# Mamba-2 mixer, two-layer decoder: the steps that read a projection's finished PSUM bank get a scheduling priority of 60

## The chip, the cores and the metric

One Trainium2 chip; the kernel runs on one core. The metric is the device time of the whole kernel in microseconds (us), the median over several runs; lower is better. TensorE (PE) multiplies matrices into PSUM, VectorE (DVE) and ScalarE (ACT) work element by element on PSUM and SBUF, GpSimd (POOL) on SBUF, and SyncE (SP) issues most DMAs.

## The reference

A two-layer decoder trunk, 2048 tokens of width 1024, float32. Layer 1 is a Mamba-2 mixer, layer 2 latent attention, each with a residual add; a final norm follows. Only the mixer bears on the change:

```python
proj = h @ w_in
z, xBC, dt_raw = jnp.split(proj, [D_INNER, D_INNER + CONV_DIM], axis=-1)
xBC = jax.nn.silu(causal_depthwise_conv(xBC, conv_w, conv_b))
...
y = ssd_chunked_scan(xh, dt, A, Bm, Cm)          # 4 groups of 8 heads, chunk by chunk
y = y + D_skip[:, None] * xh
y = y * jax.nn.silu(z)
y = y * lax.rsqrt(jnp.mean(y * y) + EPS) * g_out  # the mean per group
return y @ w_out                                  # added to h
```

D_INNER is 2048 and the groups are 4, so the mixer has an input projection of 1024 to 5152 columns and an output projection of 2048 to 1024.

## The kernel before

**Tiling.** The tokens are cut into 4 blocks of 512 (b) and the inner width into 4 groups of 512 (g). `mamba()` walks the 16 items (b, g). For an item it runs the scan `ssd(b, g)` in four chunks of 128 tokens, and beside it, as generators that are stepped in turn with the scan's 20 steps, the projections that surround it: `outp` of the item before (its output projection), `xbc` (the convolution's input) and `zgate` (the gate) of the next item. So the projections' matmuls fill TensorE while the scan's chain of small steps runs on the other engines.

**A projection.** `sweep()` fills banks of PSUM, tag "mm", of which there are four in all. For each product of two 128-row factors `mm3` (L401, L402, L403) issues three f16 or fp32r matmuls (high x high, high x low, low x high). The first two products run bank by bank, the middle ones product by product, and the last two bank by bank again; right after a bank's last matmul `evacuate(bank, i)` is called. The next projection's first matmul into a bank must wait until `evacuate` has read it. There are three such functions:

- in `xbc`, L1054: a ScalarE copy (with a scale) of the bank into `craw`; GpSimd saves three columns (L1055), ScalarE and VectorE compute the convolution into `cacc` (L1058, three times L1060) and the SiLU into `xs` or `BC` (L1062, L1063)
- in `zgate`, L1089 and L1090: a ScalarE Tanh of the bank into `sz`, then a VectorE product of `sz` and the bank
- in `outp`, L1119: a VectorE product of the bank and `rr`, added to the residual `hs`. `outp` does this twice, for the column halves n = 0 and n = 1; at the boundary between the two the four banks of n = 0 are read by four such steps, and n = 1 starts into the same banks.

**The scan's steps, per chunk.** `big` holds the decay matrix E (loaded by a DMA, L1235 and L1236 on ScalarE); VectorE multiplies it by `CB` (L1237) and makes `Xd` (L1245, with a priority of 20) and the first part of `y` (L1248) from the transposed `xs` (L1242 on TensorE). ScalarE makes `Xw` (L1251), ScalarE and GpSimd `Xp` (L1206, L1207). Then TensorE computes L1258 (32 small matmuls from `Xd` and `big`) and L408 to L410 (from `Sp`, `Ct` and from `Xp`, `Bt`). PSUM tag "tr" serves these, with four banks of its own.

**What sets the order.** A tile scheduler puts every instruction into its engine's queue. It goes by priority, which is the place in the program's text, and by its own estimate of when operands are there; an engine then works its queue in order. Inside `with tc.high_priority(n)` instructions get a priority of n places further ahead. Before the change the weights' loads and splits (`wunit`, `wpair`, `opair`: ScalarE L439, VectorE L440) have 10 (`AHEAD`) and `Xd` has 20.

Of the kernel before, what the change touches and what calls it, by code (L numbers as in the profile page):

```python
# [16 lines left out]
AF = mybir.ActivationFunctionType  # L17
ALU = mybir.AluOpType
# [366 lines left out]
class Net:  # L385
# [631 lines left out]
    def xbc(self, b, g):  # L1017

        nc, w_in, xT = self.nc, self.a["ssm_w_in"], self.xT[b]
        outs = []  # L1020
        for chans, tag, bufs in (([16 + g, 20 + g], "BC", 4), ([4 * g + j for j in range(4)], "xs", 8)):
            banks = [self.t(self.pp, "mm", [P, TB], bufs=4) for _ in chans]

            def load(k, raw):
                rows = slice(k * P, (k + 1) * P)
                if tag == "xs":
                    nc.sync.dma_start(raw, w_in[rows, DI + g * 512:DI + (g + 1) * 512])
                else:
                    both = w_in[rows, DI + DI:DI + DI + 1024].rearrange("p (n q c) -> p n q c", n=2, q=G)
                    nc.sync.dma_start(raw[:, :256].rearrange("p (n c) -> p n c", n=2), both[:, :, g, :])  # L1030

            def weights(k):
                n = 512 if tag == "xs" else 256
                if b:
                    return self.wpair(b, g, 1024 if tag == "xs" else 2048, n, k, load)
                with self.tc.high_priority(AHEAD):
                    raw = self.t(self.wp, "wraw", [P, TB], bufs=WRAW)
                    load(k, raw)
                    w = self.t(self.wp, "wsp", [P, 2, TB], F32R, bufs=WSP)
                    w = [w[:, i, :n] for i in range(2)]  # L1040
                    at = 3 * g + (1 if tag == "xs" else 2)
                    nc.scalar.activation(w[1], raw[:, :n], AF.Square, accum_out=self.nrm[:, k, at:at + 1])
                    self.split(*w, raw[:, :n])
                return w

            def product(bank, k, i, w, start, stop):
                s = slice(i * P, (i + 1) * P)
                self.mm3(bank, w[0][:, s], w[1][:, s], xT[k][:, 0, :], xT[k][:, 1, :], start, stop)

            def evacuate(bank, i):  # L1050
                ch = chans[i]
                raw = self.t(self.sp, "craw", [P, TB + 3], bufs=3)
                nc.gpsimd.tensor_copy(raw[:, 0:3], self.halo[:, ch, :])
                nc.scalar.activation(raw[:, 3:], bank, AF.Copy, scale=self.un if b else 1.0)  # L1054
                nc.gpsimd.tensor_copy(self.halo[:, ch, :], raw[:, TB:TB + 3])  # L1055
                acc = self.t(self.sp, "cacc", [P, TB], bufs=2)
                wk = [self.cw[:, 4 * ch + k:4 * ch + k + 1] for k in range(4)]
                nc.scalar.activation(acc, raw[:, 0:TB], AF.Identity, scale=wk[0], bias=self.cb[:, ch:ch + 1])  # L1058
                for k in range(1, 4):
                    nc.vector.scalar_tensor_tensor(acc, raw[:, k:k + TB], wk[k], acc, ALU.mult, ALU.add)  # L1060
                o = self.t(self.sp, tag, [P, TB], bufs=bufs)
                nc.scalar.activation(o, acc, AF.Tanh)  # L1062
                nc.vector.scalar_tensor_tensor(o, o, 1.0, acc, ALU.add, ALU.mult)  # L1063
                outs.append(o)

            yield from self.sweep(KD, banks, weights, product, evacuate)
        self.conv[b, g] = outs

    def zgate(self, b, g):

        nc, xT = self.nc, self.xT[b]
        banks, out = [self.t(self.pp, "mm", [P, TB], bufs=4) for _ in range(4)], []

        def load(k, raw):
            nc.sync.dma_start(raw, self.a["ssm_w_in"][k * P:(k + 1) * P, g * 512:(g + 1) * 512])

        def weights(k):
            if b:
                return self.wpair(b, g, 0, 512, k, load)
            return self.wunit(self.a["ssm_w_in"][k * P:(k + 1) * P, g * 512:(g + 1) * 512], 512,  # L1080
                              norm=self.nrm[:, k, 3 * g:3 * g + 1])

        def product(bank, k, i, w, start, stop):
            s = slice(i * P, (i + 1) * P)
            self.mm3(bank, xT[k][:, 0, s], xT[k][:, 1, s], *w, start, stop)

        def evacuate(bank, i):
            sz = self.t(self.sp, "sz", [P, TB], bufs=SZ)
            nc.scalar.activation(sz, bank, AF.Tanh, scale=self.unh if b else 0.5)  # L1089
            nc.vector.scalar_tensor_tensor(sz, sz, 1.0, bank, ALU.add, ALU.mult)  # L1090
            out.append(sz)

        yield from self.sweep(KD, banks, weights, product, evacuate)
        self.sz[b, g] = out

    def outp(self, b, g):

        nc, a, t0 = self.nc, self.a, b * TB
        if g == 0:
            self.hs[b] = [self.t(self.hh, "hs", [P, D], bufs=4) for _ in range(4)]  # L1100
            for i in range(4):
                nc.sync.dma_start(self.hs[b][i], a["x"][t0 + i * P:t0 + (i + 1) * P, :])
        hs, yT, rr = self.hs[b], self.yT.pop((b, g)), self.rr.pop((b, g))
        for n in range(2):
            banks = [self.t(self.pp, "mm", [P, TB], bufs=4) for _ in range(4)]

            def weights(j):
                if b:
                    return self.opair(b, g, n, j)
                r0, at = g * 512 + j * P, 4 * g + j  # L1110
                return self.wunit(a["ssm_w_out"][r0:r0 + P, n * 512:(n + 1) * 512], 512,
                                  self.go[:, at:at + 1], self.nrmw[:, 2 * at + n:2 * at + n + 1])

            def product(bank, j, i, w, start, stop):
                self.mm3(bank, yT[i][:, 0, j, :], yT[i][:, 1, j, :], *w, start, stop)

            def evacuate(bank, i):
                hv = hs[i][:, n * 512:(n + 1) * 512]
                nc.vector.scalar_tensor_tensor(hv, bank, rr[:, i:i + 1], hv, ALU.mult, ALU.add)  # L1119

            yield from self.sweep(4, banks, weights, product, evacuate)
        if g == G - 1:
            for i in range(4):
                nc.sync.dma_start(self.h_d[t0 + i * P:t0 + (i + 1) * P, :], hs[i])
# [832 lines left out]
```

## Time and profile before

| what | value |
| --- | --- |
| median of 3 runs | 2937.92 us (2934.6 to 2940.88) |
| the profiled run's own time | 2937.34 us |
| span of the profiled execution | 2935.6 us |
| mean granted TensorE clock | 0.993 |
| mixer | about 0 to 1640 us of the span |
| TensorE busy in the mixer | 1554.33 of 1640 us |
| VectorE, ScalarE busy in the mixer | 1276.16, 1088.72 us |

The profile is one execution. A row of the timeline gives the start in us, the duration, the engine, the line, the operation, output and inputs, and in brackets how long the engine stood before it and for what. Matmuls are pipelined, so their durations overlap: in a row of them each starts 0.215 us after the one before, although a row shows 0.38. Also on VectorE a next instruction starts a little before the row of the one before ends; the start-to-start distance is what an instruction takes of the queue. A view of waits gives, for a line, what it waited for, the total, the number of times and the longest.

### The profile page before, as it was taken

Reading aid. Unit: us, or ns where it says so; the run is one execution under the profiler, and the core shown is the slowest. Engines: PE = TensorE matmul, PEld = TensorE weight load, DVE = VectorE, ACT = ScalarE, POOL = GpSimd, SP = SyncE. Lnnn points to the kernel's source line nnn. Section 1 sums busy time; section 2 is a strip of 40 time slices with the busy share of each in tenths; the row PEclk is TensorE's granted clock in tenths of the full one; section 3 lists DMA queues with packets and bytes.
Section 4 is the critical chain, followed back from the end, with each engine's and each line's share of the span. In section 5 each row is a group of like instructions: output and inputs, shape, how many; then the busy total and the mean of one; then the engine's idle time right before and its main releaser. Section 6 shows DMA issues by size and latency. Waiting matters only on the chain.

```text
span 2935.6 us, 48796 instructions
## 1 busy us (share of the span) xinstructions
PE 2818.1 (96%) x16346; PEld 1652.4 (56%) x16346; DVE 2195.7 (75%) x4751; ACT 1865.0 (64%) x4728; POOL 987.4 (34%) x1200
## 2 busy tenths in 40 slices
PE   7999999989999999999999999999999999998998
PEld 6787755444444444444455555454555555554687
DVE  6778888888877777788766653644888889887575
ACT  7888777665766555566554442433888888887322
POOL 1222112212111221221111221222888888878300
PEclk9999999999999999999999999999999999999999
DMA  6333346656557545476444765555999999998894
GB/s 186 91 118 97 103 157 219 193 175 195 169 155 245 160 123 153 125 227 192 132 145 131 250 198 171 177 184 181 180 182 179 181 191 183 175 200 176 197 273 146
DMA packets 602144, 507.56 MB, mean 173 GB/s; under 512 B 413954, under 2 KB 455938, under 8 KB 601892
## 3 DMA queue, kind: packets, MB, share of 16 engines
q1 hardware_dynamic: 590020, 466.03, 60.8%
q0 software_dynamic: 11872, 38.41, 3.7%
q8 instruction: 128, 2.10, 0.3%
q14 instruction: 124, 1.02, 0.1%
HBM read 303.37 MB, written 104.47 MB: 139 GB/s over the span
## 4 chain that ended last, share of the span: by engine, by line
PE 60%; DVE 15%; ACT 8%; DMA 7%; issue 6%; POOL 3%; SPq 1%; ACTq 0%; POOLq 0%; DVEq 0%
PE mm L401 11%; PE mm L403 11%; PE mm L402 11%; PE tr L401 4%; PE tr L1717 4%; PE tr L403 4%; PE tr L402 4%; DVE cacc L1060 4%; DMA wraw<-in_ssm_w_in_dram 2%; PE mm L1690 2%; PE mm L1717 1%; PE tr L1258 1%; DMA big<-cumT 1%; PE tr L1690 1%; DVE wsp L440 1%
## 5 line engine op out<-in xcount | busy, mean ns | idle before, releaser
L1682 POOL TENSOR_TENSOR HL<-Pr,HL 128x512 f16<-128x512 f32 x320 | 371.0, 1159 | 25.5
L401 PE MATMUL mm<-xT,wsp 128*128 128x512 f16 (+1 forms) x800 | 309.5, 387 | 6.7 <-DVE sz L1090 5.1
L402 PE MATMUL mm<-xT,wsp 128*128 128x512 f16 (+1 forms) x800 | 307.2, 384 | 0.0
L403 PE MATMUL mm<-xT,wsp 128*128 128x512 f16 (+1 forms) x800 | 306.1, 384 | 0.7 <-DVE wsp L432 0.5
L1207 POOL TENSOR_TENSOR Xp<-Xw,Xp 128x512 fp32r<-128x512 f32 x64 | 87.2, 1363 | 561.6 <-ACT Xp L1206 538.6
L1676 ACT ACTIVATE Pr<-mm,nm 128x512 f32<-128x512 f32 (+3 forms) x356 | 221.1, 625 | 65.1 <-DVE nm L1671 52.9
L1665 DVE TENSOR_REDUCE mx<-mm 128x1 f32<-128x512 f32 (+3 forms) x356 | 211.6, 608 | 32.5 <-PE mm L403 18.2
L401 PE MATMUL mm<-wsp,xT 128*128 128x512 f16 (+2 forms) x640 | 233.6, 366 | 1.1 <-ACT craw L1054 0.6
L402 PE MATMUL mm<-wsp,xT 128*128 128x512 f16 (+2 forms) x640 | 233.2, 365 | 1.0 <-DVE wsp L440 1.0
L403 PE MATMUL mm<-wsp,xT 128*128 128x512 f16 (+2 forms) x640 | 232.9, 364 | 0.0
L1060 DVE SCALAR_TENSOR_TENSOR cacc<-craw,pack,cacc 128x512 f32<-128x512 f32 x288 | 220.6, 784 | 11.6 <-ACT cacc L1058 9.9
L1681 POOL CAST HL<-Pr 128x512 f16<-128x512 f32 x320 | 196.2, 613 | 95.1 <-ACT Pr L1676 94.1
L401 PE MATMUL mm<-wsp,yT 128*128 128x512 f16 (+1 forms) x512 | 199.0, 389 | 15.3 <-ACT craw L1054 8.0
L1235 ACT ACTIVATE big<-big,d_cum 128x128 f32<-128x128 f32 x512 | 169.7, 391 | 52.0 <-DMA big<-cumT 51.9
L402 PE MATMUL mm<-wsp,yT 128*128 128x512 f16 (+1 forms) x512 | 197.4, 386 | 0.3 <-DVE wsp L440 0.3
L403 PE MATMUL mm<-wsp,yT 128*128 128x512 f16 (+1 forms) x512 | 196.9, 385 | 0.0
L403 PEld LDWEIGHTS <-xT 128*128 128x128 f16 (+1 forms) x1280 | 124.7, 97 | 117.5 <-issue 2.9
L402 PEld LDWEIGHTS <-xT 128*128 128x128 f16 (+1 forms) x1280 | 125.6, 98 | 112.5 <-issue 16.9
L401 PEld LDWEIGHTS <-xT 128*128 128x128 f16 (+1 forms) x1280 | 125.1, 98 | 108.9 <-issue 17.4
L1251 ACT ACTIVATE Xw<-tr,d_wend 128x64 f32<-128x64 f32 x512 | 112.1, 328 | 111.1 <-DVE y L1248 98.2
L1676 ACT ACTIVATE Pr<-tr,nm 128x512 f32<-128x512 f32 (+3 forms) x284 | 174.1, 618 | 8.9 <-DVE nm L1671 7.9
L1665 DVE TENSOR_REDUCE mx<-tr 128x1 f32<-128x512 f32 (+3 forms) x284 | 166.1, 596 | 17.8 <-PE tr L1650 13.6
(504 smaller groups left out, 7552.7 us busy)
## 6 DMA issues: line engine op xcount, KB each, us to landing
wsp<-w_d SPq DMA_DIRECT2D x68, 512.0 KB, 3.8
wraw<-in_ssm_w_in_dram SPq DMA_DIRECT2D x128, 256.0 KB, 3.1
big<-cumT SPq DMA_DIRECT2D x64, 512.0 KB, 4.2
wraw<-in_ssm_w_out_dram SPq DMA_DIRECT2D x64, 256.0 KB, 3.1
w_d<-wsp SPq DMA_DIRECT2D x32, 512.0 KB, 3.5
wsp<-wo_d SPq DMA_DIRECT2D x32, 512.0 KB, 4.1
st<-w_d SPq DMA_DIRECT2D x56, 256.0 KB, 2.9
wsp<-wu_d SPq DMA_DIRECT2D x28, 512.0 KB, 3.8
```

The source lines that it names most:

```text
L401: mm(out, l_hi, r_hi, start=start, stop=False)
L402: mm(out, l_hi, r_lo, start=False, stop=False)
L403: mm(out, l_lo, r_hi, start=False, stop=stop)
L1060: nc.vector.scalar_tensor_tensor(acc, raw[:, k:k + TB], wk[k], acc, ALU.mult, ALU.add)
L1235: act(E[:, h, :], E[:, h, :], AF.Relu, bias=ncum[:, h0 + h:h0 + h + 1])
L1251: act(Xw[:, hc], px[:, hc], AF.Copy, scale=wend[:, h0 + h:h0 + h + 1])
L1665: v.tensor_reduce(m[:, at:at + 1], s, AX.X, ALU.max, negate=True)
L1676: nc.scalar.activation(tile("Pr", n, j, c)[:, :w], bank("S", n, j, c)[:, :w], AF.Exp, bias=moves[(4 * n + j) % len(moves)], accum_out=sums ...
L1681: nc.gpsimd.tensor_copy(u[:, 0], x)
L1682: nc.gpsimd.tensor_tensor(u[:, 1], x, u[:, 0], ALU.subtract)
L1690: nc.tensor.transpose(bank("T", n, k)[:, j * P:(j + 1) * P], tile("Pr", n, j, k // 4)[:, k % 4 * P:(k % 4 + 1) * P], self.ident)
L1717: nc.tensor.matmul(o, weights, half(n, k, low), start=start, stop=not left[n][at[0]])
```

## The change

The steps that read the bank are put in `high_priority(60)`: the ScalarE copy of the convolution's input, the Tanh and the product of the gate, the residual. Nothing else of the functions is touched, and no computing instruction is added or removed, only semaphore events change. Lines behind the change have numbers 1 to 3 higher (L1119 is now L1122, L1237 L1240, L1245 L1248, L1258 L1261).

```diff
--- before.py
+++ after.py
@@ -1051,7 +1051,8 @@
                 ch = chans[i]
                 raw = self.t(self.sp, "craw", [P, TB + 3], bufs=3)
                 nc.gpsimd.tensor_copy(raw[:, 0:3], self.halo[:, ch, :])
-                nc.scalar.activation(raw[:, 3:], bank, AF.Copy, scale=self.un if b else 1.0)
+                with self.tc.high_priority(60):
+                    nc.scalar.activation(raw[:, 3:], bank, AF.Copy, scale=self.un if b else 1.0)
                 nc.gpsimd.tensor_copy(self.halo[:, ch, :], raw[:, TB:TB + 3])
                 acc = self.t(self.sp, "cacc", [P, TB], bufs=2)
                 wk = [self.cw[:, 4 * ch + k:4 * ch + k + 1] for k in range(4)]
@@ -1086,8 +1087,9 @@
 
         def evacuate(bank, i):
             sz = self.t(self.sp, "sz", [P, TB], bufs=SZ)
-            nc.scalar.activation(sz, bank, AF.Tanh, scale=self.unh if b else 0.5)
-            nc.vector.scalar_tensor_tensor(sz, sz, 1.0, bank, ALU.add, ALU.mult)
+            with self.tc.high_priority(60):
+                nc.scalar.activation(sz, bank, AF.Tanh, scale=self.unh if b else 0.5)
+                nc.vector.scalar_tensor_tensor(sz, sz, 1.0, bank, ALU.add, ALU.mult)
             out.append(sz)
 
         yield from self.sweep(KD, banks, weights, product, evacuate)
@@ -1116,7 +1118,8 @@
 
             def evacuate(bank, i):
                 hv = hs[i][:, n * 512:(n + 1) * 512]
-                nc.vector.scalar_tensor_tensor(hv, bank, rr[:, i:i + 1], hv, ALU.mult, ALU.add)
+                with self.tc.high_priority(60):
+                    nc.vector.scalar_tensor_tensor(hv, bank, rr[:, i:i + 1], hv, ALU.mult, ALU.add)
 
             yield from self.sweep(4, banks, weights, product, evacuate)
         if g == G - 1:
```

What the scheduler makes of it: on VectorE 73 of the 128 residuals and 12 of the 64 gate products move forward, 23 of 64 `Xd` and 25 of 64 `big` move back; on ScalarE 47 of 96 copies and 13 of 64 Tanh move forward. TensorE's order changes where VectorE's does.

**VectorE at the boundary from n = 0 to n = 1 of the item at 600 to 611 us of the profile (block 1).** `hs` with the four numbers is the four residuals, `cacc` and `xs` the next item's convolution, `Xd`, `big` and `y` the scan's chunk. Before:

```order
L1060 SCALAR_TENSOR_TENSOR cacc_6398<-craw_6394,pack,cacc_6398 128x512
L1245 TENSOR_TENSOR Xd_6480<-tr_6475,d_dt_3869 128x512
L1063 SCALAR_TENSOR_TENSOR xs_6385<-xs_6385,cacc_6380 128x512
L1060 SCALAR_TENSOR_TENSOR cacc_6398<-craw_6394,pack,cacc_6398 128x512
L1237 TENSOR_TENSOR big_6440<-big_6440,CB_6451 128x1024
L1060 SCALAR_TENSOR_TENSOR cacc_6398<-craw_6394,pack,cacc_6398 128x512
L1248 TENSOR_TENSOR y_6483<-tr_6475,pack 128x512
L1119 SCALAR_TENSOR_TENSOR hs_6406<-mm_6414,rr_5918,hs_6406 128x512
L1063 SCALAR_TENSOR_TENSOR xs_6403<-xs_6403,cacc_6398 128x512
L1119 SCALAR_TENSOR_TENSOR hs_6407<-mm_6415,rr_5918,hs_6407 128x512
L1119 SCALAR_TENSOR_TENSOR hs_6408<-mm_6416,rr_5918,hs_6408 128x512
L1119 SCALAR_TENSOR_TENSOR hs_6409<-mm_6417,rr_5918,hs_6409 128x512
```

After:

```order
L1122 SCALAR_TENSOR_TENSOR hs_6406<-mm_6414,rr_5918,hs_6406 128x512
L1064 SCALAR_TENSOR_TENSOR xs_6385<-xs_6385,cacc_6380 128x512
L1061 SCALAR_TENSOR_TENSOR cacc_6398<-craw_6394,pack,cacc_6398 128x512
L1122 SCALAR_TENSOR_TENSOR hs_6407<-mm_6415,rr_5918,hs_6407 128x512
L1061 SCALAR_TENSOR_TENSOR cacc_6398<-craw_6394,pack,cacc_6398 128x512
L1122 SCALAR_TENSOR_TENSOR hs_6408<-mm_6416,rr_5918,hs_6408 128x512
L1236 TENSOR_TENSOR CB_6451<-tr_6442,pack 128x128
L1064 SCALAR_TENSOR_TENSOR xs_6403<-xs_6403,cacc_6398 128x512
L1122 SCALAR_TENSOR_TENSOR hs_6409<-mm_6417,rr_5918,hs_6409 128x512
L1248 TENSOR_TENSOR Xd_6480<-tr_6475,d_dt_3869 128x512
L1240 TENSOR_TENSOR big_6440<-big_6440,CB_6451 128x1024
```

The four residuals stood behind `Xd`, `big` and `y`, and now stand ahead of them.

**TensorE at the same place.** `mm_1184` is the last bank of n = 0, `mm_1204` to `mm_1207` are the banks of n = 1, `tr_1201` is the scan's L1258 and `tr_1202` its L408 to L410. Before:

```order
L403 LDWEIGHTS yT_1023_5539
L403 MATMUL mm_1184_6417<-wsp_1197_6493,yT_1023_5539 128x512
L1258 MATMUL tr_1201_6534<-Xd_1194_6480,big_1188_6440 64x64 x16
L408 MATMUL tr_1202_6552<-Sp_1159_6299,Ct_1191_6448 128x512
L409 MATMUL tr_1202_6552<-Sp_1159_6299,Ct_1191_6448 128x512
L410 MATMUL tr_1202_6552<-Sp_1159_6299,Ct_1191_6448 128x512
L401 LDWEIGHTS yT_952_5138
L401 MATMUL mm_1204_6559<-wsp_1208_6563,yT_952_5138 128x512
L402 LDWEIGHTS yT_952_5138
```

After, the last rows of the third bank of n = 1 and what follows it:

```order
L402 LDWEIGHTS yT_1023_5539
L402 MATMUL mm_1206_6561<-wsp_1208_6563,yT_1023_5539 128x512
L403 LDWEIGHTS yT_1023_5539
L403 MATMUL mm_1206_6561<-wsp_1208_6563,yT_1023_5539 128x512
L1261 MATMUL tr_1201_6534<-Xd_1194_6480,big_1188_6440 64x64 x16
L408 MATMUL tr_1202_6552<-Sp_1159_6299,Ct_1191_6448 128x512
L409 MATMUL tr_1202_6552<-Sp_1159_6299,Ct_1191_6448 128x512
L410 MATMUL tr_1202_6552<-Sp_1159_6299,Ct_1191_6448 128x512
L401 LDWEIGHTS yT_1023_5539
```

L1258 (now L1261) stood at the boundary itself; now the 18 matmuls of the banks `mm_1204`, `mm_1205` and `mm_1206` stand between the last matmul of n = 0 and it.

**VectorE at the next item's boundary, 702 to 708 us.** The names are as in the first place. Before:

```order
L1063 SCALAR_TENSOR_TENSOR xs_7418<-xs_7418,cacc_7413 128x512
L1060 SCALAR_TENSOR_TENSOR cacc_7431<-craw_7427,pack,cacc_7431 128x512
L1233 TENSOR_TENSOR CB_7498<-tr_7489,pack 128x128
L1060 SCALAR_TENSOR_TENSOR cacc_7431<-craw_7427,pack,cacc_7431 128x512
L1237 TENSOR_TENSOR big_7487<-big_7487,CB_7498 128x1024
L1063 SCALAR_TENSOR_TENSOR xs_7436<-xs_7436,cacc_7431 128x512
L1119 SCALAR_TENSOR_TENSOR hs_6406<-mm_7449,rr_6916,hs_6406 128x512
L1245 TENSOR_TENSOR Xd_7553<-tr_7548,d_dt_3869 128x512
L1119 SCALAR_TENSOR_TENSOR hs_6407<-mm_7450,rr_6916,hs_6407 128x512
L1119 SCALAR_TENSOR_TENSOR hs_6408<-mm_7451,rr_6916,hs_6408 128x512
```

After:

```order
L1061 SCALAR_TENSOR_TENSOR cacc_7431<-craw_7427,pack,cacc_7431 128x512
L1061 SCALAR_TENSOR_TENSOR cacc_7413<-craw_7409,pack,cacc_7413 128x512
L1122 SCALAR_TENSOR_TENSOR hs_6406<-mm_7449,rr_6916,hs_6406 128x512
L1061 SCALAR_TENSOR_TENSOR cacc_7431<-craw_7427,pack,cacc_7431 128x512
L1064 SCALAR_TENSOR_TENSOR xs_7418<-xs_7418,cacc_7413 128x512
L1122 SCALAR_TENSOR_TENSOR hs_6407<-mm_7450,rr_6916,hs_6407 128x512
L1064 SCALAR_TENSOR_TENSOR xs_7436<-xs_7436,cacc_7431 128x512
L1122 SCALAR_TENSOR_TENSOR hs_6408<-mm_7451,rr_6916,hs_6408 128x512
L1122 SCALAR_TENSOR_TENSOR hs_6409<-mm_7452,rr_6916,hs_6409 128x512
L432 TENSOR_TENSOR Bt_7492<-tr_7489,Bt_7492 128x128
L1236 TENSOR_TENSOR CB_7498<-tr_7489,pack 128x128
L1248 TENSOR_TENSOR Xd_7553<-tr_7548,d_dt_3869 128x512
```

The first residual stood behind `CB` and `big` and now stands ahead of both and of `Bt`, with the other three between `xs` and `cacc`; `Xd` and `big` come after all four.

**VectorE near 428 to 440 us.** `wsp` is a weight pair's split for the gate; the pair has a first split from one `wraw` and a second from the next. Before, the pair's two splits:

```order
L440 SCALAR_TENSOR_TENSOR wsp_4715<-wraw_4716,rw,wsp_4715 128x512
L1063 SCALAR_TENSOR_TENSOR xs_4568<-xs_4568,cacc_4563 128x512
L1060 SCALAR_TENSOR_TENSOR cacc_4581<-craw_4577,pack,cacc_4581 128x512
L440 SCALAR_TENSOR_TENSOR wsp_4715<-wraw_4720,rw,wsp_4715 128x512
L1060 SCALAR_TENSOR_TENSOR cacc_4581<-craw_4577,pack,cacc_4581 128x512
```

After, the second of them (from `wraw_4720`):

```order
L1248 TENSOR_TENSOR Xd_4702<-tr_4697,d_dt_310 128x512
L1064 SCALAR_TENSOR_TENSOR xs_4615<-xs_4615,cacc_4610 128x512
L1064 SCALAR_TENSOR_TENSOR xs_4633<-xs_4633,cacc_4628 128x512
L1240 TENSOR_TENSOR big_4662<-big_4662,CB_4673 128x1024
L1251 TENSOR_TENSOR y_4705<-tr_4697,pack 128x512
L440 SCALAR_TENSOR_TENSOR wsp_4715<-wraw_4720,rw,wsp_4715 128x512
```

The second split stood two places behind the first in the middle of the convolution, and now stands behind `Xd`, `xs`, `big` and `y`.

## The prediction

> **What bounds the kernel now.** I read the page first: the share of each engine, then the chain that ended last.
>
> ```profile
> PE 2818.1 (96%) x16346; PEld 1652.4 (56%) x16346; DVE 2195.7 (75%) x4751; ACT 1865.0 (64%) x4728; POOL 987.4 (34%) x1200
> PE 60%; DVE 15%; ACT 8%; DMA 7%; issue 6%; POOL 3%; SPq 1%; ACTq 0%; POOLq 0%; DVEq 0%
> ```
>
> TensorE is busy 96% of 2935.6 us, so what an order can win is the time in which it stands. The change touches the mixer alone, about 0 to 1640 us. The view of waits for TensorE from 60 to 1500 us (columns: instruction, what it waited for, us in total, times, longest) gives the prices:
>
> ```profile
> PE tr L410 <- POOL Xp L1207: 12.9, 18, 1.4
> PE tr L1258 <- DVE big L1237: 10.7, 6, 2.5
> PE mm L401 <- ACT craw L1054: 8.5, 7, 2.8
> PE tr L1258 <- issue: 7.6, 6, 2.5
> PE mm L401 <- DVE hs L1119: 7.0, 4, 3.3
> PE mm L401 <- DVE sz L1090: 5.1, 4, 2.3
> PE tr L1258 <- DVE Xd L1245: 3.8, 4, 1.6
> ```
>
> Three rows are the change's target, a projection that waits for a bank to be read: 8.5 + 7.0 + 5.1 = 20.6 us, 0.7% of the span. That is the ceiling of the direct gain. Three others are the scan's products (L1258), which wait for Xd and big: 10.7 + 7.6 + 3.8 = 22.1 us. These operands come from the engine that the residuals use, VectorE, and they are what the change puts behind.
>
> **The boundary between the two halves of an output projection.** There the four residuals of n = 0 free the banks of n = 1, and a chunk's L1258 stands nearby. At 607 us the timeline shows this, and the windows view the load of the 28 us around it:
>
> ```profile
> 604.68 0.38 PE L403 MATMUL mm<-wsp,yT 128*128 128x512 f16 x1
> 605.04 0.75 DVE L1060 SCALAR_TENSOR_TENSOR cacc<-craw,pack,cacc 128x512 f32<-128x512 f32 x1
> 605.71 1.22 DVE L1237 TENSOR_TENSOR big<-big,CB 128x1024 f32<-128x1024 f32 x1
> 606.84 0.74 DVE L1060 SCALAR_TENSOR_TENSOR cacc<-craw,pack,cacc 128x512 f32<-128x512 f32 x1
> 607.03 1.15 PE L1258 MATMUL tr<-Xd,big 128*64 128x64 f32 x32 [1.97 <-issue]
> 608.11 0.74 DVE L1119 SCALAR_TENSOR_TENSOR hs<-mm,rr,hs 128x512 f32<-128x512 f32 x1
> 608.76 0.68 DVE L1063 SCALAR_TENSOR_TENSOR xs<-xs,cacc 128x512 f32<-128x512 f32 x1
> 609.36 2.06 DVE L1119 SCALAR_TENSOR_TENSOR hs<-mm,rr,hs 128x512 f32<-128x512 f32 x3
> ```
>
> ```profile
> 597.00:625.00 28.00, 25.02 (x144) 12.40 (x144) 27.75 (x46) 18.35 (x42) 5.05 (x7) 1.00 0.44 135
> ```
>
> VectorE is busy 27.75 of 28 us: nothing can be put ahead there without pushing something back. From start to start a residual takes 0.66 us, cacc 0.67, xs 0.60, big 1.13. In the new order four residuals (2.64), one xs and one cacc stand ahead of Xd and big that stood behind them: 3.9 us. So big ends at 610.7 instead of 606.8. On TensorE the new order puts 18 matmuls of n = 1 ahead of L1258; matmuls in a row start 0.215 us apart (a bank's six take 1.29), so that is 3.9 us as well. TensorE stood from 604.9 to 607.03 for big; it will run 18 matmuls and stand from 608.8 to about 610.9. **Gain at 607: 0.** The wait moves, with its length.
>
> At 1001 us L1258 moves behind 11 matmuls only:
>
> ```profile
> 999.79 1.21 DVE L1237 TENSOR_TENSOR big<-big,CB 128x1024 f32<-128x1024 f32 x1
> 1001.06 1.15 PE L1258 MATMUL tr<-Xd,big 128*64 128x64 f32 x32 [1.36 <-DVE big L1237]
> 1002.13 2.71 DVE L1119 SCALAR_TENSOR_TENSOR hs<-mm,rr,hs 128x512 f32<-128x512 f32 x4
> ```
>
> Four residuals and an xs now precede the later of Xd and big, 3.24 us, against 11 x 0.215 = 2.37: **-0.9**. At the five other boundaries of this kind L1258 goes 15 to 19 matmuls back (3.2 to 4.1 us) and VectorE's delay is 3.2 to 3.9 by the same durations: between -0.7 and +0.9 each, and 0.1 in sum as I count their rows.
>
> At two boundaries the residual itself ended last. The first is the 3.28 us at 705:
>
> ```profile
> 700.65 0.28 DVE L432 TENSOR_TENSOR Bt<-tr,Bt 128x128 fp32r<-128x128 f32 x1
> 702.14 0.28 DVE L1233 TENSOR_TENSOR CB<-tr,pack 128x128 f32<-128x128 f32 x1
> 703.00 1.22 DVE L1237 TENSOR_TENSOR big<-big,CB 128x1024 f32<-128x1024 f32 x1
> 704.14 0.68 DVE L1063 SCALAR_TENSOR_TENSOR xs<-xs,cacc 128x512 f32<-128x512 f32 x1
> 704.74 0.74 DVE L1119 SCALAR_TENSOR_TENSOR hs<-mm,rr,hs 128x512 f32<-128x512 f32 x1
> ```
>
> ```profile
> 701.65 0.60 PE L1242 MATMUL tr<-pack,xs 128*128 128x128 f32 x4
> 705.53 0.38 PE L401 MATMUL mm<-wsp,yT 128*128 128x512 f16 x1 [3.28 <-DVE hs L1119]
> ```
>
> Bt (0.22), two xs (1.2), CB (0.2), a cacc (0.67) and big (1.14) go behind the first residual: it ends 3.4 us earlier, at 702.0, when TensorE is just through L1242 (702.1). The second residual then stands behind a cacc and an xs, ends at 703.9, and its matmul would start at 703.4: some 0.6 us of wait is left. **Gain +2.65.** The other is alike:
>
> ```profile
> 1091.36 0.74 DVE L1119 SCALAR_TENSOR_TENSOR hs<-mm,rr,hs 128x512 f32<-128x512 f32 x1
> 1092.16 0.38 PE L401 MATMUL mm<-wsp,yT 128*128 128x512 f16 x1 [2.10 <-DVE hs L1119]
> ```
>
> The same operations go behind it: **+2.1**. What is late next at both is big, 3.4 us later, with L1258 a bank or more further back: covered. Boundaries in sum: 2.65 + 2.1 - 0.9 + 0.1 = **+4.0**.
>
> **Convolution input and gate.** 47 of 96 craw copies move forward, past 0.6 to 1.9 us of ScalarE's work; only 13 of 64 Tanh and 12 of 64 gate products move, and three of the four waits on sz are at ones that don't. Five of the seven craw waits stand some 9 us ahead of a boundary as above, this one for example, ahead of 607:
>
> ```profile
> 597.27 0.67 ACT L1054 ACTIVATE craw<-mm,un 128x512 f32<-128x512 f32 x1
> 597.99 0.38 PE L401 MATMUL mm<-wsp,yT 128*128 128x512 f16 x1 [2.76 <-ACT craw L1054]
> ```
>
> A TensorE that passes 598 earlier meets a VectorE that still delivers big when it did; it waits there instead. Two waits are left, at the means of their rows 8.5/7 + 5.1/4 = 2.5. Bounds: 0, and all 13.6; I take **+2**, near the low end, since the cover is VectorE's 27.75 of 28.
>
> **Xp** (12.9 us in 18 waits) comes from ScalarE's Xw, past which copies move in both directions; bounds -2 and +4, taken: **+1**.
>
> **What goes back.** 46 of VectorE's weight splits (L440) move later, by 53 us in sum: their own priority is 10, now below the residuals' 60. Worst is the second split at 428.48, now behind Xd, two xs, big and y:
>
> ```profile
> 428.48 0.74 DVE L440 SCALAR_TENSOR_TENSOR wsp<-wraw,rw,wsp 128x512 f16<-128x512 f32 x1
> 436.80 1.22 DVE L1237 TENSOR_TENSOR big<-big,CB 128x1024 f32<-128x1024 f32 x1
> 438.07 1.15 PE L1258 MATMUL tr<-Xd,big 128*64 128x64 f32 x32 [2.53 <-DVE big L1237]
> ```
>
> TensorE can do all of that weight's first half and four matmuls of the second; ten that ran ahead of L1258 then follow it, while big ends no earlier: 10 x 0.215 = **-2.15** (a wait of 4.7 us instead of 2.5). At 132 us a y goes 2.3 us later:
>
> ```profile
> 132.59 0.68 DVE L1283 TENSOR_TENSOR y<-y,sz 128x512 f32<-128x512 f32 x1
> 133.41 0.63 PE L1301 MATMUL tr<-pack,y 128*128 128x128 f32 x4 [0.40 <-DVE y L1283]
> ```
>
> It had no slack, and L1301 moves only five matmuls back (1.1): **-1.1**. For the other splits I take **-0.8**, part of one split's mean delay of 1.15; bounds 0 and -4.
>
> **Other queues.** On SyncE 43 of 1514 issues change place by a few rows (a weight's load past a store or past a chunk's load of big), on GpSimd 21 of 1200, mostly copies of three columns. The stores wait for the splits just named, so a late split can hold a load behind it; no row among TensorE's waits above names a load, so I take 0, and the bounds of the splits (0 and -4) hold it.
>
> **The clock.** The windows view shows a stretch right behind the wait at 705:
>
> ```profile
> 705.84:709.25 3.41, 3.41 (x11) 1.12 (x10) 3.41 (x7) 0.51 (x3) 0.00 (x0) 0.50 0.00 0
> ```
>
> TensorE ran 3.41 us at half the clock (the 0.50), which costs up to 1.7 us. Without the wait I count **+1.5**; bounds 0 and 1.7 for each such stretch kept or lost, and a new wait like the one near 433 can bring its own. The Trainium skill ("TensorE: Matmul & The Clock Gate", Part 1: The HAM clock gate) has the clock fall after an idle window of about 3.4 us. This trace shows it behind waits shorter than that (3.28), so by the page's rule this term would be 0.
>
> **The sum.** 4.0 + 2 + 1 - 2.15 - 1.1 - 0.8 + 1.5 = 4.45 us. The profiled run took 2937.34 us (its span 2935.6); it would take 2932.9. The median of the runs is 2937.92, 0.6 above, so the forecast is **2933.5 us**, 0.15% less. About 0.2% (5.9 us) is what a measurement here can tell from no change, so the likeliest outcome lies just inside it.
>
> **The rivals.** *Slower: VectorE's queue held by residuals.* Residuals now stand ahead of Xd and big and wait in their queue for their bank. The group view has what that costs today:
>
> ```profile
> L1119 DVE SCALAR_TENSOR_TENSOR hs<-mm,rr,hs 128x512 f32<-128x512 f32 x128 | 92.3, 742 | 12.3 <-PE mm L403 12.2
> ```
>
> 12.2 us in 18 idle times is 0.7 each. If at the nine boundaries of the b > 0 items Xd and big come 0.7 later by that and 0.9 more as at 1001, 9 x 1.6 = 14.4 are lost; with the other terms but the boundaries' (+0.45) and 705 and 1092 (+4.75) kept: 9 us slower, 2947. It decides from 0.5 us more per boundary (4.45/9). For it speaks that VectorE is full there; against it that the order lets TensorE run 11 to 19 matmuls meanwhile. Chance 0.20. The Trainium skill ("PSUM — Partial Sum Buffer", Engine vs sequencer instructions) states that VectorE's queue is strictly first in, first out; by that a residual that waits holds Xd and big, whatever their data. The timeline's order at 607 agrees.
>
> *Full relief.* If the waits at the boundaries turn out to be TensorE's and not VectorE's, most of 20.6 us go, less the 4 that go back: 17 us, 2921. Against it stands the 27.75 of 28. Chance 0.13.
>
> *Nothing.* The gains before a boundary are all given back at it, and the weight splits cancel 705 and 1092: within 2 us of 2938. That the order would not change is excluded (73 of 128 residuals move). Chance 0.12.
>
> The forecast itself has 0.55: own range 2928 to 2940, by the bounds of craw, Xp and splits. It gives 0.22 faster, 0.32 same, 0.01 slower. Faster: 0.22 + 0.13 = 0.35; same: 0.32 + 0.12 = 0.44; slower: 0.01 + 0.20 = 0.21. The range for 8 in 10 reaches half into the slow case and half into full relief: 2923 to 2946.
>
> **What would show it.** Right: the row of L401 on hs falls from 7.0 to about 2, L401 on craw and sz stay above 8 together or fall while L1258's rows rise; L1258 on Xd, big and issue stays at 20 to 28; at 607 the wait stands behind the 18th matmul of n = 1; near 433 a wait of over 4 us; no half clock at 705. Wrong: L1258 under 12 (full relief), or over 32 with VectorE idle ahead of hs well above 12.2 (the slow rival), or a span that moves while these rows do not.

## The result and the profile after

The changed kernel takes 2943.03 us in the median of 20 runs (2935.25 to 2950.34), the kernel before 2938.39 in 20 runs beside them (2932.01 to 2943.28): ratio 1.0018, 95% interval 1.0010 to 1.0025. It is **slower by 4.6 us**, where 4.45 us less were forecast. The time lies within the stated range, the sign is the other one. By size the change is inside the 0.2% that the prediction took for the least it could tell from none, but its interval excludes no change. The range reached half into the slow case, so that the time fell into it is no merit of the sum.

The profiled execution of the changed kernel took 2935.25 us, the fastest of its 20 runs, with a span of 2933.5 us: by itself it would have shown a gain. Its mixer has two stretches of half clock, where the two profiles of the kernel before have six and eight. So I read it together with a second profile of the same kernel (the first experiment below, 2945.78 us, span 2944.0). TensorE's waits from 60 to 1500 us, first profile of the changed kernel (columns as in the prediction; L1258 is now L1261, L1119 L1122, L1237 L1240):

```profile
PE tr L410 <- POOL Xp L1210: 17.4, 23, 1.6
PE tr L1261 <- DVE big L1240: 8.6, 5, 3.5
PE tr L1261 <- issue: 7.2, 7, 1.8
PE mm L401 <- DVE sz L1092: 7.0, 4, 2.2
PE mm L401 <- ACT craw L1055: 6.9, 7, 1.3
PE mm L401 <- DVE hs L1122: 4.4, 8, 1.0
PE tr L1261 <- DVE Xd L1248: 4.1, 3, 1.8
```

The same rows of its second profile:

```profile
PE tr L410 <- POOL Xp L1210: 16.5, 22, 1.4
PE tr L1261 <- DVE big L1240: 9.1, 5, 3.5
PE mm L401 <- ACT craw L1055: 8.2, 9, 1.6
PE tr L1261 <- issue: 8.0, 7, 2.0
PE mm L401 <- DVE sz L1092: 7.1, 4, 2.6
PE mm L401 <- DVE hs L1122: 5.0, 9, 1.0
PE tr L1261 <- DVE Xd L1248: 5.0, 4, 2.4
```

The three rows that the change aims at were 8.5 (craw), 7.0 (hs) and 5.1 (sz), 20.6 in sum; they are 18.3 and 20.3 now. The wait on the residual is shorter, but spread over 8 or 9 places, and the wait on the gate has grown. The scan's products (L1261) wait 19.9 and 22.1, as before (22.1). The row of Xp has grown by 4 us.

Place by place the residual did what was worked out. At 705 us, TensorE in the first profile of the changed kernel:

```profile
703.23 0.60 PE L1245 MATMUL tr<-pack,xs 128*128 128x128 f32 x4
705.38 0.38 PE L401 MATMUL mm<-wsp,yT 128*128 128x512 f16 x1 [0.25 <-DVE hs L1122]
```

The wait of 3.28 is down to 0.25. At the boundary that was at 607 (here some 2 us later):

```profile
607.31 0.38 PE L401 MATMUL mm<-wsp,yT 128*128 128x512 f16 x1 [0.38 <-DVE hs L1122]
609.24 0.38 PE L401 MATMUL mm<-wsp,yT 128*128 128x512 f16 x1 [0.47 <-DVE hs L1122]
613.79 1.15 PE L1261 MATMUL tr<-Xd,big 128*64 128x64 f32 x32 [1.78 <-issue]
```

The wait ahead of the scan's products was 1.97 and is 1.78, behind the 18 matmuls, with two small waits on residuals in front: nothing won, as forecast. And near 433 to 439 us the late weight split shows, first on TensorE, then on VectorE:

```profile
432.32 0.38 PE L402 MATMUL mm<-wsp,xT 128*128 128x512 f16 x1 [0.80 <-DVE wsp L440]
439.23 1.15 PE L1261 MATMUL tr<-Xd,big 128*64 128x64 f32 x32 [3.52 <-DVE big L1240]
```

```profile
431.52 0.74 DVE L440 SCALAR_TENSOR_TENSOR wsp<-wraw,rw,wsp 128x512 f16<-128x512 f32 x1
432.18 4.06 DVE L1061 SCALAR_TENSOR_TENSOR cacc<-craw,pack,cacc 128x512 f32<-128x512 f32 x6
436.15 0.69 DVE L1248 TENSOR_TENSOR Xd<-tr,d_dt 128x512 f32<-128x512 f32 x1
437.95 1.22 DVE L1240 TENSOR_TENSOR big<-big,CB 128x1024 f32<-128x1024 f32 x1
439.69 1.41 DVE L440 SCALAR_TENSOR_TENSOR wsp<-wraw,rw,wsp 128x512 f16<-128x512 f32 x2
```

Six steps of the convolution in one piece (4.06 us) stand between the pair's first split and Xd; the second split comes at 439.69. The 2.53 us of before are 0.80 + 3.52 now. At 132 us, where the late y was to cost 1.1 us, the wait of 0.40 is 0.43:

```profile
133.78 0.63 PE L1304 MATMUL tr<-pack,y 128*128 128x128 f32 x4 [0.43 <-DVE y L1286]
```

A wait that nobody had before is on ScalarE. What its copies of the convolution's input waited for, in the kernel before and in the changed one:

```profile
  PE mm L403: 0.3, 1
```

```profile
  DVE cacc L1061: 4.4, 5
  PE mm L403: 1.1, 2
```

The copies now run so far ahead that they wait for one of the three `craw` buffers, which VectorE's convolution holds, and ScalarE's queue stands behind them.

### The profile page after: what moved, and what is told of

The parts are those of the page before. It is cut to its first block, busy times and chain, and to the rows that moved or that the text cites. A ratio compares the mean times of both kernels' runs of the same rounds, so it can differ in the third digit from the quotient of the medians.

```text
span 2933.5 us, 48819 instructions
## 1 busy us (share of the span) xinstructions
PE 2812.0 (96%) x16346; PEld 1647.6 (56%) x16346; DVE 2200.6 (75%) x4751; ACT 1861.8 (63%) x4728; POOL 977.6 (33%) x1200
## 4 chain that ended last, share of the span: by engine, by line
PE 46%; DVE 10%; DMA 6%; ACT 5%; issue 3%; POOL 3%; SPq 0%; ACTq 0%; DVEq 0%; POOLq 0%
PE mm L401 7%; PE mm L403 7%; PE mm L402 7%; PE tr L401 4%; PE tr L403 4%; PE tr L1720 4%; PE tr L402 4%; PE mm L1693 2%; DVE cacc L1061 2%; PE mm L1720 1%; PE tr L1693 1%; DMA big<-cumT 1%; DMA w_d<-wraw 1%; POOL HL L1685 1%; DMA PX<-HL 1%
## 5 line engine op out<-in xcount | busy, mean ns | idle before, releaser
L1668 DVE TENSOR_REDUCE mx<-mm 128x1 f32<-128x512 f32 (+3 forms) x356 | 211.9, 609 | 33.2 <-PE mm L403 19.9
L1061 DVE SCALAR_TENSOR_TENSOR cacc<-craw,pack,cacc 128x512 f32<-128x512 f32 x288 | 213.3, 776 | 14.8 <-ACT cacc L1059 12.9
L1238 ACT ACTIVATE big<-big,d_cum 128x128 f32<-128x128 f32 x512 | 169.7, 391 | 49.3 <-DMA big<-cumT 46.9
L1668 DVE TENSOR_REDUCE mx<-tr 128x1 f32<-128x512 f32 (+3 forms) x284 | 166.2, 597 | 18.3 <-PE tr L1653 11.5
```

The lines of the kernel that those rows point to most:

```text
L1238: act(E[:, h, :], E[:, h, :], AF.Relu, bias=ncum[:, h0 + h:h0 + h + 1])
L1668: v.tensor_reduce(m[:, at:at + 1], s, AX.X, ALU.max, negate=True)
```

## The experiments

Each kernel ran on one chip beside runs of the kernel before; ratios are to those runs, with their 95% intervals; a ratio can differ from that of the two medians by up to 0.0006. The theories: **A**, the residual wins and the copies of the convolution's input lose; **B**, first in the form that the residuals hold Xd and big back at the boundaries (my rival of the prediction), later that the copies themselves push the scan back; **C**, only the clock differs; **D**, the two stalls at 705 and 1092 are all that can be won; **F**, the late weight splits are the whole loss; **E** and **G** as the expectations say.

### The two kernels again, and each part alone

The second run of each has no edit. The other two keep one `high_priority(60)` and drop the others; of the gate's two steps alone no experiment was needed: with a priority on them only, every engine's order is that of before, row for row. Beside the residual's priority it changes no order either. In the whole change it moves steps at one place, near 322 us (below). So the residual alone and the whole change differ by the copies, but for that one place.

For the residual alone the copy's (in `xbc`) and the gate's go, for the copy alone the gate's and the residual's, each by

```diff
-                with self.tc.high_priority(60):
+                if True:
```

> The changed kernel once more, for a second profile beside one that happened to be the fastest of its runs. All theories: 2943 us, 0.1 to 0.25% above before, clock about 0.993. Theory A (TensorE's waits grew, by what the copies of the convolution's input push back): the waits of TensorE on Xp are again above 15 us (12.9 before), the wait for big near 438 us is again over 4 us, the stall at 705 is again gone. Theory C (only the clock differs): the sum of waits is that of before within 3 us, and there are 3 or more half-clock stretches of 3.41 us more than before.

Measured: 2946.59 us against 2940.64, **1.0022** (1.0013 to 1.0031), clock 0.993 in the mean of its 12 runs (0.9924 in 35 of before). Waits on Xp 16.5, the wait for big 3.52, 0.4 us of wait on a residual near 705 (3.28 before). TensorE's waits from 60 to 1500 us sum to 73.3 us (68.6 in the first profile of the change, 66.9 and 67.8 in the two of before). In the mixer this profile has 3.41 us of half clock six times (one stretch is of 6.83), the two profiles of before six and eight times: theory C falls.

> The order of before once more (with the line numbers of the changed kernel), as the null: ratio 1.000 within 0.1%, and a second profile of the same order, which tells how much the waits by line and the number of half-clock stretches differ from run to run with nothing changed. If the waits on Xp lie between 12 and 14 us again, a change of 4 us in that row means something; if they spread over 5 us, it does not.

Measured: 2939.87, **0.9999** (0.9991 to 1.0008). Xp 13.9 (12.9 in the first profile), hs 7.6 (7.0), craw 8.7 (8.5): the rows repeat within 1.5 us.

> Only the residual has the priority of 60. Its order keeps the second weight split at 428 us where it was and moves L1258 back by 11 to 19 matmuls at the boundaries, as the whole change does. Theory A (the convolution's copy costs, the residual gains): the terms of the boundaries alone, +4.0 and up to +1.5 of clock: 2933 to 2935 us, faster than before by 0.1 to 0.2%. Theory B (the slow rival: residuals hold Xd and big back at the boundaries): 2942 to 2947, as slow as the whole change or slower. Theory C (only the clock differs): 2938 at equal clock.

Measured: 2937.60 against 2940.64, **0.9984** (0.9975 to 0.9992): faster by 3.0 us by the medians, 4.7 by the ratio. Theory B in its first form falls. That this is the boundaries' +4.75 is less sure than the number: their waits are gone (hs 3.0), but Xp grows to 19.2, and the sum of TensorE's waits is 66.4 where before had 66.9 and 67.8. The mean clock of its runs is 0.9940 against 0.9924; 0.0016 of 2940 us is 4.7 us.

> Only the copy of the convolution's input has the priority of 60. Its order holds the second weight split at 428 us behind Xd, big and y, the y at 132 us 2.3 us later, and 100 of ScalarE's Xw products earlier; L1258 stays where it was at all but one boundary. Theory A: the losses of the whole change without its gains: 2944 to 2949 us, slower by 0.2 to 0.4%, TensorE's waits on Xp above 15 us. Theory B (the boundaries cost): 2936 to 2939, as before. Theory C (only the clock differs): 2938 at equal clock.

Measured: 2943.43, **1.0010** (1.0001 to 1.0018): slower, by less than expected, and Xp was 11.7, not above 15. So A holds in sign, but 0.9984 and 1.0010 don't make 1.0022: together they cost some 6 us (by the medians) to 8 us (by the ratios) more than apart. One overlap is seen at 1092 us, where before TensorE waited 2.10 us: with the copy alone it waits

```profile
1090.19 0.38 PE L401 MATMUL mm<-wsp,yT 128*128 128x512 f16 x1 [0.24 <-DVE hs L1122]
1092.59 0.38 PE L401 MATMUL mm<-wsp,yT 128*128 128x512 f16 x1 [0.94 <-DVE hs L1122]
```

(L1122 is not prioritized in this kernel.) An earlier convolution shortens the queue ahead of the residual as well; the two edits win part of the same stall. At 705 us it is alike: with the copy alone 2.3 of the 3.28 us are left. That makes some 2 of the 6 to 8 us.

Another loss is only in the whole change (1.84 us in its second profile): at 322 us TensorE waits for a gate product that has the priority of 60.

```profile
322.25 0.50 PE L401 MATMUL mm<-wsp,yT 128*128 128x512 f32 x1 [1.75 <-DVE sz L1092]
```

ScalarE's Tanh of that bank, first before, then in the changed kernel:

```profile
318.18 0.58 ACT L1089 ACTIVATE sz<-mm 128x512 f32<-128x512 f32 x1
318.74 0.63 ACT L1206 ACTIVATE Sp<-st 128x512 fp32r<-128x512 f32 x1
```

```profile
318.89 0.63 ACT L1209 ACTIVATE Sp<-st 128x512 fp32r<-128x512 f32 x1 [1.53 <-DVE st L1279]
...
320.13 0.57 ACT L1091 ACTIVATE sz<-mm 128x512 f32<-128x512 f32 x1
```

The prioritized step stands behind Sp and a weight's step now. Without the gate's priority ScalarE has the order of before here in the changed kernel too, so the gate's priority does this, together with the copies'. Why the scheduler puts a step with more priority later is not shown; I take it that its own estimate of when the bank is full has shifted.

### Smaller doses, and earlier weights

The residual alone at 20, and the whole change at 20 (all three places):

```diff
-                with self.tc.high_priority(60):
+                with self.tc.high_priority(20):
```

The residual alone, for n = 1 only:

```diff
-                with self.tc.high_priority(60):
+                with self.tc.high_priority(60 if n == 1 else 0):
```

The whole change with the weights at 70:

```diff
-AHEAD = 10
+AHEAD = 70
```

> Only the residual, with a priority of 20 in place of 60. Its order puts L1258 behind 18 matmuls at two boundaries (705 and 1092 us), where TensorE waited for the residual, and leaves it at the seven others. Theory D (two stalls are all there is to win, and each of the other moved boundaries and each late split costs): it keeps the gains at 656 to 713 us (about -5.5) and 1095 to 1121 (-2.9) and drops the losses of the residual alone at 594, 771, 1173 and 1350 us (+1.5 to +2.4 each): ratio 0.997 to 0.998, at least as fast as the residual at 60 (0.9984). Theory E (any earlier residual helps by freeing banks): half of the gain of 60 at most, 0.999.

Measured: 2933.04 against 2938.94, **0.9980** (0.9971 to 0.9988). The L1261 rows sum to 22.0 (22.1 before) and the waits on the residual are 0.8 in sum: the two stalls are gone, and the sum of TensorE's waits from 60 to 1500 us falls to 64.7 (66.9 and 67.8 before). D holds.

> Only the residual, at 60, and only for the second column half (n = 1), which frees banks for the next item's projection. No boundary from n = 0 to n = 1 is moved. Theory D: the gains at 701 to 713 and 1095 to 1121 us are gone, as n = 0 carries them; the stall of 3.3 us at 705 is there again; 0.999 to 1.000. Theory E: as good as the residual whole, 0.9984.

Measured: 2938.02, **0.9999** (0.9989 to 1.0008): D holds, E falls. The residual's gain is that of n = 0. One part of the expectation failed: near 705 us the wait on the residual is 1.4 us, not 3.3, while those on the copies around it grew from 1.8 to 4.2.

> The whole change with 20 in place of 60. The order moves only the boundaries at 705 and 1092 us, but keeps the late second split at 428 us (9.35 us later) and the y at 132 us. Theory D: the gains at 656 to 713 and 1095 to 1121 us (together about -8), the losses of the convolution's copy at 103 to 160, 427 to 458 and 568 to 594 us (+0.5, +2, +1), none of those of the residual at 320, 594, 771, 984 and 1350: between the copy alone (1.001) and the residual alone (0.9984), so 0.999 to 1.001, and under the whole change at 60 (1.0022) by 3 us or more. Theory B (the copies themselves are what costs): 1.001 to 1.002.

Measured: 2944.33, **1.0022** (1.0013 to 1.0031), as slow as at 60. Theory D's reckoning of the copies' losses was too small; B in its second form (the copies cost) is right. At 20 the copies never wait for a `craw` buffer (no row of cacc), so that wait of ScalarE is not what costs here.

> The whole change at 60, and the weights' loads and splits at 70 in place of 10, so that no split stands behind an evacuation or a scan step. The second split at 428 us keeps its place (0.14 us later, the first 3.3 us earlier). Theory D: the loss at 427 to 458 us (1.4 to 2.2) is gone, those at 320, 771 and 1350 us stay; splits this early can push Xd, big and y later instead (VectorE is full), so the sum is 1.000 to 1.002. Theory F (the late splits are the whole loss): the ratio falls to that of the residual alone, 0.9984.

Measured: 2932.31, **0.9981** (0.9971 to 0.9991). That looked like F. But it lacks a control: the weights' priority alone.

### What the weights' priority does alone, and where the copies cost

The kernel before with `AHEAD = 70`; the copy alone with it; the whole change with copies prioritized in blocks 2 and 3 only, weights at 10; the residual at 20 with `AHEAD = 70`. The edit of the third, in `xbc`:

```diff
-                with self.tc.high_priority(60):
+                with self.tc.high_priority(60 if b >= 2 else 0):
```

> The kernel before with the weights' loads and splits at 70 in place of 10 and no priority on the evacuations: what the priority of the weights does by itself. Theory F (the whole change loses because its evacuations stand ahead of the weight splits; splits early enough are no better than splits on time): 0.999 to 1.001, so the 0.9981 of the whole change with the splits at 70 is the evacuations' own gain. Theory G (an early weight is worth something by itself, and the evacuations add nothing to it): 0.998, the same as with them.

Measured: 2928.00 against 2937.74, **0.9962** (0.9948 to 0.9975). The weights' priority is worth 0.38% alone; with the change it is 0.9981. So the change still costs about 0.2% where no split is late: F falls as the whole cause. G holds in its first half, an early weight is worth something by itself; the evacuations do not leave that gain as it is, they cost half of it.

> Only the copy of the convolution's input at 60, with the weights at 70. Alone, with the weights at 10, it was 1.001. Theory F: the loss at 100 to 600 us (3.7 us in its profile) is gone and what it won at 656 to 713 and 1095 to 1121 us stays: 0.998 to 0.9995. Theory B (the copies cost by what else they push back: E's steps, Xw): 1.000 to 1.001 still.

Measured: 2937.61, **0.9999** (0.9991 to 1.0008): the copies cost 0.37% on top of early weights. B.

> The whole change, except that the copy of the convolution's input has its priority only in blocks 2 and 3, whose weights come ready from memory and need no splits; weights at 10. The second split at 428 us and the y at 132 us keep their places. Theory F (the loss is the splits' at 100 to 600 us, 5.6 to 7.7 us in the two profiles of the change): 0.998 to 0.999, like the residual alone. Theory B: the copies lose in blocks 2 and 3 too (+1.5 at 1039, +3 at 1276, +1.8 at 1350 us), 1.000 to 1.0015.

Measured: 2935.79, **0.9994** (0.9984 to 1.0003). Of the distance from the residual alone (0.9984) to the whole change (1.0022 in the second measurement) some three quarters, 0.28%, is the copies' in blocks 0 and 1, where weights are split; the last quarter is inside the intervals.

> The residual alone at 20 (0.998 with the weights at 10) and the weights at 70: the two best single settings together. Theory F: the residual at 20 has no late split to lose by, so the weights' priority adds little: 0.997 to 0.998. Theory G: both gains add, 0.996. If the early splits push Xd, big and y later (VectorE is full): 0.999.

Measured: 2924.52 against 2937.74, **0.9950** (0.9937 to 0.9962). Both gains add, nearly; this version beats both kernels.

### The copies alone, once more

Still open was what the copies cost by. The residual at 60 with `AHEAD = 70`, without the copies; and the whole change with only block 1's weight pairs at 70 (`wpair` and `opair`):

```diff
-            with self.tc.high_priority(AHEAD):
+            with self.tc.high_priority(70 if b == 1 else AHEAD):
```

> The residual at 60 and the weights at 70, no priority on the copies: against the whole change with the weights at 70 (0.9981) it differs by the copies alone. If the copies cost even where no split is late (theory B), 0.994 to 0.996, since the weights alone give 0.9962 and the residual alone 0.9984. If the copies cost only by the splits they push back (theory F), 0.998, the same as with them.

Measured: 2926.94 against 2940.57, **0.9956** (0.9943 to 0.9969); with the copies it was 0.9981. The copies cost 0.25% with early splits too: B.

> The whole change, and only those weights at 70 that are split in block 1 (the pairs of both projections); block 0's and the ready weights of blocks 2 and 3 stay at 10. Theory F (the late splits of block 1 are the loss): as good as with all weights at 70, 0.998, and TensorE's waits from 100 to 600 us fall from 24 to under 20. Theory B (the copies push back E, Xd and the convolution too): 1.000 to 1.001, the waits from 600 to 1600 us stay at 50.

Measured: 2934.54, **0.9981** (0.9971 to 0.9990). Block 1's early splits alone bring as much as all weights at 70; the waits from 100 to 600 us fall to 18.9, those from 600 to 1600 stay high (54.3). F is right for the first stretch, B for the second. Block 1's early splits without the copies did not run, so part of the 0.4% can be what early weights are worth by themselves.

Sums over all rows of TensorE's waits, one profile each, show stretches apart; the copies are the difference within a pair. The mixer's weight splits reach into the second stretch (L440 on wsp runs to 902 to 917 us), so its part from 930 us, behind the last of them, stands by itself:

| kernel | 100 to 600 us | 600 to 1600 us | of these, from 930 us |
| --- | --- | --- | --- |
| before, two profiles; the copies alone | 20.7, 20.9; 22.5 | 48.4, 49.3; 50.3 | 25.1, 26.0; 28.7 |
| residual at 60; with copies (the change, two profiles) | 20.6; 24.5, 23.7 | 48.1; 48.3, 52.2 | 26.5; 30.0, 29.6 |
| residual at 20; with copies at 20 | 18.0; 25.2 | 49.7; 51.5 | 25.8; 27.2 |
| weights at 70; with copies | 18.3; 18.5 | 49.5; 55.5 | 26.6; 28.2 |
| residual at 60, weights at 70; with copies | 16.4; 15.4 | 47.3; 50.7 | 28.0; 29.7 |
| residual at 60; with copies in blocks 2 and 3 | 20.6; 18.4 | 48.1; 52.9 | 26.5; 30.0 |

In the first stretch the copies cost 3 to 7 us beside the residual (under 2 alone) while the splits are late, and nothing when the splits stand ahead or the copies stay back. Before, its rows on big and on splits are

```profile
PE tr L1258 <- DVE big L1237: 5.2, 3, 2.5
PE mm L402 <- DVE wsp L440: 1.0, 1, 1.0
PE mm L401 <- ACT wsp L439: 0.5, 1, 0.5
```

and in the changed kernel's second profile

```profile
PE tr L1261 <- DVE big L1240: 6.2, 3, 3.5
PE mm L402 <- DVE wsp L440: 2.5, 3, 1.6
PE mm L401 <- DVE sz L1092: 1.8, 1, 1.8
PE mm L401 <- ACT wsp L439: 1.8, 2, 0.9
```

while with all weights at 70 the rows of wsp are gone and big is

```profile
PE tr L1261 <- DVE big L1240: 1.2, 1, 1.2
```

In the second stretch the copies cost 0 to 6 us beside the residual or early weights, where the two profiles of the change differ by 3.9. From 930 us on, where no split of the mixer is left to be late, they cost 1.4 to 3.6 us in every pair, and two profiles of one kernel differ by 0.9 at most: late splits are not the whole of it. The waits that grow there are of two kinds. Beside a residual at 60 they are those on the gate and the residual (sz 1.5 and hs 1.4 become 3.8 and 2.7 in the change); without it they are L1261's (9.0 and 9.3 become 12.4 with the copies alone). By the order an earlier copy brings the convolution's VectorE steps forward with it: from the residual alone to the whole change, 98 of 288 go to an earlier place and 52 to a later one, while 35 of 131 weight splits go later and Xd and big move both ways (19 earlier, 9 later). That this is the price is argued, not shown. No experiment held the convolution back with the copies early.

## Why the prediction was wrong, step by step

The sum was 4.45 us to the good and the runs show 4.6 to the bad (6 in the second measurement): 9 to 10.5 us lie between. Step by step:

- **The ceiling and the boundaries** (+4.0, with 705 at +2.65, 1092 at +2.1, 1001 at -0.9, 607 at 0): right place by place. 3.28 us became 0.25, the 2.10 at 1092 is gone in the change, the 1.36 at 1001 became 1.78, and 607 kept its wait. The residual alone, which carries these terms, is faster by 3.0 to 4.7 us. That this meets the sum is in part luck: its waits fall by 0.5 to 1.4 us in all, as Xp takes back what the stalls give, and the rest is of the size of its higher clock. At 20, where the residual moves the two stalls' boundaries and none of the other seven, it is faster by 0.20%, and its waits fall by 2 to 3 us.
- **The clock** (+1.5): the stretch of half clock at 705 is gone in both profiles, and the mean clock of all runs is 0.9930 against 0.9924, 0.0006 of 2940 us or 1.8 us. Right in size for these runs; but the clock moves with each edit (0.9940 with the residual alone, 0.9909 with the copies alone, 0.9915 with the change at 20), and one stretch at 705 does not account for that. By the page of the Trainium skill that the prediction set against it ("TensorE: Matmul & The Clock Gate", Part 1: The HAM clock gate) the term would have been 0; the stretch stood behind a wait of 3.28 us in both profiles of before, so the measurement decides.
- **What goes back** (-2.15 at 438, -1.1 at 132, -0.8): the first place is there (2.53 became 0.80 + 3.52), the second is not (0.40 became 0.43). The third term was undersized: I priced 45 other late splits as part of one. With the copies back in blocks 0 and 1 only, the change gains 0.28% or 8 us, and making block 1's splits early gains 0.4%, though early weights are worth something by themselves. All three together were 4.05 us.
- **Convolution input and gate** (+2): **the step that failed.** It took the copy as free where it moves, since a TensorE that passes 598 earlier would only wait at the boundary instead, and set the bounds at 0 and 13.6, with no loss. I had counted how far each copy jumps on ScalarE (0.6 to 1.9 us), not what follows it: each copy has four steps of the convolution behind it on the two engines, which come forward with it. The measured price of the copies is +0.10% alone and +0.25 to +0.42% beside the residual or early weights, 3 to 12 us. In the prediction the copies stood at +2 here and at -4.05 in what goes back, 2 us of loss; beside the residual they measured 9 us (2937.60 against 2946.59) to 11 (by the ratios). Those 7 to 9 us are most of the miss. The gate's priority did nothing but at 322, where it lost 1.8 us.
- **Xp** (+1): the sign was wrong, 12.9 became 17.4 and 16.5. But the residual alone has 19.2 there and is faster, and the copies alone have 11.7: as I read it, a TensorE that arrives earlier waits there longer. Then that row is a place where gains are given back, not a price of its own.
- **The rivals**: the slow one came true in sign at 0.20, by another mechanism than the one written. Residuals in VectorE's queue were innocent: its idle time ahead of them is

```profile
L1122 DVE SCALAR_TENSOR_TENSOR hs<-mm,rr,hs 128x512 f32<-128x512 f32 x128 | 94.2, 745 | 12.4 <-PE mm L403 12.2
```

against 12.3 before (14.1 in the second profile of the change, 10.9 with the residual alone).

## What to carry to other kernels

When a priority moves a step, price what the step draws forward behind it and what it pushes back on each engine, not the step: a copy takes 0.67 us, and moving 47 of them ahead cost 3 to 12 us in sum. Before giving evacuations the right of way, see whether the next weights have it: raising the weights' priority alone was worth twice the best setting of the evacuations, and the residual did as well at 20, where it moves only the boundaries of the two stalls, as at 60. And before any theory of the whole change, run it with each part left out: that is the control that told the residual from the copies.

## What the hardware showed that I had not expected

The time of one program spreads by 15 us over 20 runs (2935 to 2950), and in the changed kernel that goes with the granted clock: the run at 0.989 took 2949.24 us, the one at 0.991 2950.34, those at 0.995 took 2935.25 to 2939.93; the correlation over the 20 runs is -0.85, and a line through them gives 2.2 us for each 0.001 of clock. It is not as close in every kernel: 35 runs of the kernel before have -0.37 and 1.0 us. In the mixer the clock's records are stretches of 3.41 or 6.83 us at one half, nearly all at or right behind a single wait of TensorE of 1.7 to 4.7 us. Whether a wait has one behind it changes from run to run: 1.75 us at 322 had none in the first profile of the change, 1.84 in the second had one; the 3.52 us near 439 had none in the first, 6.83 us in the second and 3.41 with the copies alone. So one profile of each kernel, 2 us apart the wrong way round, could not show a difference of 5 us in the median; the rows of waits, which repeat within 1.5 us, could show where to look.
